# Keeping x on chip after the first mixer, turning some of its quarters through DRAM, and another order of the last HGRN head groups

## The chip, the cores and the metric

The kernel runs on one core of one Trainium2 chip. The metric is the time of one execution on the device in microseconds (us). The program does its matrix products on TensorE (PE), element-wise work on VectorE (DVE) and ScalarE (ACT), small work and part of the transfers on GpSimd (POOL), and issues the weight transfers from SyncE (SP). SBUF is the memory on the chip, PSUM the memory that TensorE writes into, and DRAM the memory beside the chip.

## What is computed

A trunk of two layers on 256 rows of 2048 columns, all in float32. Layer 0 mixes the rows with a gated DeltaNet (GDN), layer 1 with HGRN2; each mixer is followed by a SwiGLU feed-forward block (FFN) with 5632 inner columns. Each of the four sub-layers normalizes its input by rows and adds its result to x:

```python
h = x
for layer in range(DEPTH):
    if layer % N_MIXERS == 0:
        h = h + gdn_mixer(rmsnorm(h, gdn_norm[j]), gdn_w_in[j], gdn_conv[j], gdn_a_log[j], ...)
    else:
        h = h + hgrn2_mixer(rmsnorm(h, hgrn_norm[j]), hgrn_w_in[j], lb_table[layer], ...)
    h = h + swiglu(rmsnorm(h, ffn_norm[layer]), ffn_w_gate[layer], ffn_w_up[layer], ffn_w_down[layer])
return rmsnorm(h, final_norm)

def swiglu(h, w_gate, w_up, w_down):
    return (jax.nn.silu(h @ w_gate) * (h @ w_up)) @ w_down

def hgrn2_mixer(h, w_in, lower_bound, head_norm, w_out):
...
    o = hgrn2_chunked(q, k, i, logf).astype(h.dtype)
    o = rmsnorm(o, head_norm) * jax.nn.silu(gate)
    return o.reshape(B, S, HGRN_VAL_DIM) @ w_out
```

## The kernel before

**Weights and the main stream.** All weights are read once, as halves of 128x1024 float32 (512 KB), by SP's queue into `raw`. Each half is split into two numbers of lower precision: ACT writes the rounded part `wh`, DVE the rest `wl` (`load` in `stream`, lines 610 to 623). The activations are split likewise (`xt_h` and `xt_l` for the input of a sub-layer, `ot_h` and `ot_l` for the output of a mixer, `hth` and `htl` inside the FFN), and a product is formed as xh·wh + xh·wl + xl·wh. One half so feeds twelve matmuls of 128x512, called *main* below. Halves are loaded three ahead and have four buffers at each step.

**Groups.** A `Group` is a run of halves that add up into one PSUM tile, with a function `end` that takes the result out. In order of time: the GDN mixer with its out projection, FFN 0, the HGRN mixer with its out projection, FFN 1. An FFN is 12 gate-and-up groups of 96 mains, four down groups of 144 mains (one for each quarter of 512 columns of x), 10 more gate-and-up groups, and four down groups of 120 mains. HGRN takes its 16 heads in four head groups; each has the groups f, q, v and z of 96 mains, in the order f0 q0 v0 z0 f1 ... z3 (lines 1638 and 1639). An out projection is done in parts (four for GDN, two for HGRN); each part is four groups of 48 mains, one for each quarter. The part p reads head groups 2p and 2p+1, the first in the first 24 mains of a group and the second in the last 24.

**x and the boundaries.** x lives in DRAM as `x_home`. Where a group adds to a quarter of it, `load_x` (line 777) brings the quarter into one of two buffers, `add_x` (line 781) adds the PSUM tile on DVE, and the quarter is stored again; both transfers are POOL's. At the three boundaries (GDN to FFN 0, FFN 0 to HGRN, HGRN to FFN 1) `next_input` (line 789) then makes the input of the next sub-layer from each quarter: `make_xt` (line 731) does eight transposes of 128x128 on TensorE into PSUM, four splits on ACT (`xt_h`, with the norm's weight as scale) and four on DVE (`xt_l`); `sumsq` (line 696) sums the squares on ACT. The row scale of the norm is applied later, behind the products.

**Turning through DRAM.** In HGRN and in the FFN a second way to transpose is in use, `turn` (line 751): DVE turns all 32x32 blocks of a 128x1024 tile, POOL stores the result to DRAM (`rows`), and four loads of POOL bring it back with the blocks at their places (`turned`). HGRN's f and q come through it (`blocks_in`, `rows_in`), and so does the output of a head group (`head_out`, line 1207): `zs` gets the gated output, is turned by way of the buffer of `v`, and is split into `ot_h` and `ot_l`, which have three buffers.

**HGRN's work beside the stream.** `hgrn_scores` (line 1452) makes the score tile `sc` and the tile `cross` of a head group with some 30 element-wise steps and small matmuls; `hgrn_o` (line 1589) multiplies them with `v`, and `head_out` follows.

**What sets the order.** Nothing is issued as it is written. `Recorder.add` collects all operations, and `plan` (line 311) puts them in order with a model: a cost for each operation (`COST`), landing times for transfers, and a latest time for each, counted back from those that use it. The main matmuls keep the order in which they were written. The others are placed between them by their latest time; small matmuls and transposes (tiles called `aux`) go between mains where the model has their inputs ready with a slack of 1.5 us. Each engine then works in the planned order and waits in it, POOL with its transfers too. All operations are issued by one line, 502, so the profile names them by their tiles.

Of the kernel before, what the change touches and what calls it, by code (L numbers as in the profile page):

```python
# [8 lines left out]
F32 = mybir.dt.float32  # L9
F32R = mybir.dt.float32r  # L10
U8 = mybir.dt.uint8
AF = mybir.ActivationFunctionType
ALU = mybir.AluOpType
# [4 lines left out]
P = 128  # L18
# [7 lines left out]
N_HGRN = 4  # L26
# [9 lines left out]
    "k0 k1 k2 k3 v0 v1 z0 z1 v2 z2 k4 k5 v3 z3 v4 k6 o0 k7 v5 z4 z5 o1 v6 v7 z6 z7 o2 o3"  # L36
)

# [477 lines left out]
class Trunk:  # L519
# [211 lines left out]
    def make_xt(self, cg, norm):  # L731
# [11 lines left out]
        for pair, ps in enumerate(two):  # L743
            for k in range(2):
# [3 lines left out]
                    self.norms[:, norm, 4 * cg + kt : 4 * cg + kt + 1],  # L748
                )

    def turn(self, x, blocks, turned, by_head=False):

        nc = self.nc
        width = x.shape[1] // 4
        if by_head:
            b, rows = (x.rearrange(e, t=2, n=4, c=4) for x, e in ((blocks, "p (c n t j) -> p t n c j"), (x, "p (t n c i) -> p t n c i")))
            for tt in range(2):
                nc.vector.transpose(b[:, tt], rows[:, tt])
        else:
            nc.vector.transpose(  # L760
                blocks.rearrange("p (c a j) -> p a c j", c=4, j=32), x.rearrange("p (a c i) -> p a c i", c=4, i=32)
            )
        rows = self.tile(self.dram, [4, P, width], f"rows{width}", bufs=3)
        nc.gpsimd.dma_start(rows.rearrange("c p a -> p c a"), blocks.rearrange("p (c a) -> p c a", c=4))
        for c in range(4):
            nc.gpsimd.dma_start(
                turned[32 * c : 32 * c + 32].rearrange("i (q a) -> i q a", q=4),
                rows[c].rearrange("(q i) a -> i q a", q=4),
            )
        return turned  # L770

    def x_cols(self, x, cg):
        if x is self.a["x"]:
            return x[cg]
        return x.rearrange("(t p) c -> p t c", p=P)[:, :, cg * 512 : (cg + 1) * 512]

    def load_x(self, cg):
        self.x[cg] = self.tile(self.xpool, [P, 2, 512], "x", ordered=True)
        self.nc.gpsimd.dma_start(self.x[cg], self.x_cols(self.x_at, cg))

    def add_x(self, ps, cg, keep=True):
        x = self.x[cg]
        self.nc.vector.tensor_tensor(out=x, in0=x, in1=ps, op=ALU.add)
        if keep:
            self.nc.gpsimd.dma_start(self.x_cols(self.x_home, cg), x)
        if cg == 3:
            self.x_at = self.x_home

    def next_input(self, norm, row):


        def after(cg):
            self.make_xt(cg, norm)
            self.sumsq(cg)
            if cg == 3:
                self.make_rstd(row)

        return after
# [3 lines left out]
    def ffn(self, j, after):  # L802
        nc, a = self.nc, self.a
        hts = {}

        def gate_up(gi):
            def end(ps):
                h1 = self.tile(self.pool, [P, 2, T], "h1", bufs=4)
                for tt in range(2):
                    col = self.rstd[:, tt : tt + 1]  # L810
                    sg = self.tile(self.pool, [P, T], "sg", bufs=2)
                    nc.scalar.activation(sg, ps[:, tt, 0:T], AF.Silu, scale=col)
                    nc.vector.scalar_tensor_tensor(
                        out=h1[:, tt, :], in0=ps[:, tt, T:512], scalar=col, in1=sg,
                        op0=ALU.mult, op1=ALU.mult,
                    )
                blocks = self.tile(self.pool, [P, 512], "blocks", bufs=2)
                flat = h1.rearrange("p t c -> p (t c)")
                turned = self.turn(flat, blocks, flat).rearrange("p (q a j) -> p a q j", q=4, j=32)
                hts[gi] = ht, lt = tuple(  # L820
                    self.tile(self.pool, [P, 2, 2, P], f"ht{x}", F32R, bufs=max(FF_PARTS)) for x in "hl"
                )
                as_turned = lambda x: x.rearrange("p t n (q j) -> p (t n) q j", q=4)
                nc.scalar.activation(as_turned(ht), turned, AF.Copy)
                nc.vector.tensor_tensor(
                    out=as_turned(lt), in0=turned, in1=as_turned(ht.bitcast(F32)), op=ALU.subtract
                )

            gu = a[f"ffn_gu{j}"]
            return Group(  # L830
                [gu[gi, i] for i in range(4)],
                lambda ps, i, h, l: self.mm_rows(ps, i, h, l, 4, self.operand), end,
            )

        def down(part, cg):
            first = sum(FF_PARTS[:part])
            n = FF_PARTS[part] // 2
            w = a[f"ffn_d{j}_{part}"]

            def operand(kt):  # L840
                h, l = hts[first + kt // 2]
                return h[:, :, kt % 2, :], l[:, :, kt % 2, :]

            last = part == len(FF_PARTS) - 1
            apart = last and j == 1 and cg == 3

            def end(ps):
                if apart:
                    self.finish_last(ps)
                    return  # L850
                self.add_x(ps, cg, not (last and j == 1))
                if last:
                    after(cg)

            mm = self.mm_apart if apart else self.mm_rows
            return Group(
                [w[cg, i] for i in range(n)],
                lambda ps, i, h, l: mm(ps, i, h, l, n, operand), end,
                lambda: self.load_x(cg), apart,
            )  # L860

        groups = []
        for part, n in enumerate(FF_PARTS):
            lo = sum(FF_PARTS[:part])
            groups += [gate_up(gi) for gi in range(lo, lo + n)]
            groups += [down(part, cg) for cg in range(4)]
        groups[0].begin = lambda: self.enter(f"ffn{j}")
        return groups


# [5 lines left out]
    def gdn_setup(self):  # L876
        nc, a = self.nc, self.a
        self.enter("gdn")
        t = lambda shape, tag, dt=F32: self.tile(self.pool, shape, tag, dt)
        self.conv = t([P, 32, 4], "conv")  # L880
        nc.gpsimd.dma_start(self.conv, a["gdn_conv"])
        self.gate_in = t([64, 2], "gate_in")
        nc.gpsimd.dma_start(self.gate_in, a["gdn_gate"])
        self.gdn_hn = t([P, 33], "gdn_hn")[:, 0:1]
        nc.gpsimd.dma_start(self.gdn_hn, a["gdn_hn"])
        self.unit = t([P, 8, 32], "unit")
        nc.gpsimd.dma_start(self.unit, a["unit"])
        self.expo = t([P, 4], "expo")
        nc.gpsimd.memset(self.expo[:, 0:4:2], 0.5)
        nc.gpsimd.memset(self.expo[:, 1:4:2], -0.5)  # L890
        self.resets = self.tile(self.pool, [64, T], "sq", bufs=2)
        nc.gpsimd.memset(self.resets, 1.0)
        nc.gpsimd.memset(self.resets.rearrange("p (c s) -> p c s", s=CH)[:, :, 0:1], 0.0)
        zero = self.tile(self.pool, [3, 512], "w", bufs=2)
        nc.gpsimd.memset(zero, 0.0)
        self.v_rows = [self.tile(self.dram, [T + 3, 512], f"v_rows{i}", bufs=1) for i in range(2)]
        for rows in self.v_rows:
            nc.gpsimd.dma_start(rows[0:3, :], zero)
        self.gates = t([P, 2, 64], "gates")
        self.shift = t([P, 32, 6], "shift")  # L900
        self.g_rows = self.tile(self.dram, [32, T], "g_rows", bufs=1)
        self.g_tots = self.tile(self.dram, [32, 4], "g_tots", bufs=1)
# [454 lines left out]
    def out_proj(self, name, p, states, last, after):  # L1357
# [8 lines left out]

        def make(cg):
            def end(ps):
                self.add_x(ps, cg)
                if last:  # L1370
                    after(cg)

# [13 lines left out]
    def hgrn_setup(self):  # L1386
        nc, a = self.nc, self.a
        self.enter("hgrn")
        t = lambda shape, tag, dt=F32: self.tile(self.pool, shape, tag, dt)
        self.hgrn_hn = t([P, 25], "hgrn_hn")[:, 0:1]  # L1390
        nc.gpsimd.dma_start(self.hgrn_hn, a["hgrn_hn"])
# [60 lines left out]
    def hgrn_scores(self, g, rows, st):  # L1452
        nc = self.nc
# [29 lines left out]
        for h in range(4):  # L1483
            nc.tensor.matmul(
                ps[:, h * P : (h + 1) * P], kp[:, h, 0:P], qp[:, h, :], start=True, stop=True
            )
        cross = t([P, 512], "cross")
        nc.scalar.activation(cross, ps, AF.Copy)
        st["cross"] = cross

        sc = t([P, 8, P], "sc")
        nc.gpsimd.memset(sc, 0.0)

        sides = (slice(0, CH), slice(CH, P))
# [112 lines left out]
    def hgrn(self, after):  # L1607
# [27 lines left out]
            )  # L1635
            return [rows(1, f_end), rows(0, q_end), rows(2, v_end), rows(3, z_end)]

        for g in range(N_HGRN):
            groups += part(g)
        groups[0].begin = self.hgrn_setup  # L1640
        groups += self.out_proj("hgrn_out", 0, states, False, after)
        groups += self.out_proj("hgrn_out", 1, states, True, after)
# [53 lines left out]
    def run(self):  # L1696
        self.setup()
        self.start(0, True)
        groups = self.gdn(self.next_input(1, False))
        groups += self.ffn(0, self.next_input(2, False))  # L1700
        groups += self.hgrn(self.next_input(3, False))
        groups += self.ffn(1, self.finish)
        self.stream(groups)
        self.leave()

    def enter(self, name):

        self.leave()
        self.pool = self.nc.pool(name, 1, phase=True)

    def leave(self):
        if self.pool:
# [83 lines left out]
```

## Time and profile before

| what | value |
|---|---|
| median of 3 runs | 2775.16 us (2774.61 to 2776.39) |
| the profiled execution, its own time | 2773.76 us |
| its span, first to last instruction | 2772.0 us |
| TensorE transposes of x (`aux<-head,x`) | 112, of these 96 at the boundaries |
| DMA, mean over the span | 222 GB/s, 616.00 MB |
| software queue (POOL's transfers) | 109.48 MB, 13.1% of 16 engines' span |

The profile is one execution on the chip. Its page gives the busy time of each engine, a picture of the span in 40 slices, the queues, the chain of waits that ended last, and the costliest groups of instructions. A group's row names engine, operation, the tile written and the tiles read, the shape, the count, the busy time in us, the mean of one in ns, and the idle time before them with what ended it. In the timeline a row is start, duration, engine, operation, and in brackets the idle time before it and what ended that. PE's matmuls overlap, so their pace is read from start to start. The clock of TensorE is given as a share of full speed.

### The profile page before, as it was taken

What the parts mean: (1) busy time and instruction counts of PE and PEld (TensorE: products, weight loads), DVE (VectorE), ACT (ScalarE), POOL (GpSimd) and SP (SyncE); (2) the same over time, 40 slices, a digit from 0 to 9 for tenths busy, and PEclk for the clock granted to TensorE, in tenths of its full rate; (3) what the DMA queues carried; (4) which work ended last, traced back from release to release, by engine and by line L of the source; (5) the groups of instructions that cost most, each with busy time, mean ns of one, the idle gap of its engine ahead of it and who ended that gap; (6) DMA issues with size and microseconds to landing.
All of it is one profiled execution on the core that took longest, in us unless ns stands there. A gap on an engine that the chain in (4) does not pass through costs nothing.

```text
span 2772.0 us, 39544 instructions
## 1 busy us (share of the span) xinstructions
PE 2753.7 (99%) x14730; PEld 2312.3 (83%) x14730; DVE 1765.3 (64%) x2571; ACT 1435.5 (52%) x2028; POOL 414.2 (15%) x646
## 2 busy tenths in 40 slices
PE   9999999999999999999999999999999999999998
PEld 9988988887888888888888888888788888888887
DVE  6787888878755555445555576787755555455554
ACT  6656666565554444434444466566454444344443
POOL 1212222232111111001110101101111111011100
PEclk9999999999999999999999999999999999999999
DMA  7686668677777667766666767567787667676664
GB/s 256 197 279 209 205 232 265 214 231 240 237 236 227 215 217 221 226 224 216 220 216 223 232 194 224 192 186 229 231 264 217 218 215 226 221 223 217 218 215 159
DMA packets 175841, 616.00 MB, mean 222 GB/s; under 512 B 24618, under 2 KB 25786, under 8 KB 175520
## 3 DMA queue, kind: packets, MB, share of 16 engines
q1 hardware_dynamic: 138912, 503.15, 56.4%
q0 software_dynamic: 36448, 109.48, 13.1%
q8 instruction: 115, 1.88, 0.3%
q10 hardware_dynamic: 288, 0.85, 0.1%
q14 instruction: 78, 0.64, 0.1%
HBM read 568.25 MB, written 45.13 MB: 221 GB/s over the span
## 4 chain that ended last, share of the span: by engine, by line
PE 98%; DVE 1%; ACT 0%; issue 0%; POOLq 0%; POOL 0%; DVEq 0%; ACTq 0%
PE main L502 92%; PE aux L502 7%; DVE wl L502 0%; ACT dec L502 0%; ACT wh L502 0%; DVE ot_l L502 0%; DVE zs L502 0%; DVE utmp L502 0%; DVE u L502 0%; DVE x L502 0%; ACT y L502 0%; ACT xt_h L502 0%; POOLq L1792 0%; ACT junk L502 0%; DVE xl L502 0%
## 5 line engine op out<-in xcount | busy, mean ns | idle before, releaser
L502 DVE TENSOR_TENSOR wl<-raw,wh 128x1024 fp32r<-128x1024 f32 x945 | 1157.6, 1226 | 914.2 <-ACT wh L502 907.0
L502 ACT ACTIVATE wh<-raw 128x1024 fp32r<-128x1024 f32 x945 | 1000.7, 1060 | 1230.3 <-PE main L502 1180.1
L502 PE MATMUL main<-wh,xt_l 128*128 128x512 f32 x2432 | 949.9, 391 | 0.0
L502 PE MATMUL main<-wl,xt_h 128*128 128x512 f32 x2432 | 948.2, 390 | 1.3 <-DVE wl L502 1.3
L502 PE MATMUL main<-wh,xt_h 128*128 128x512 f32 x2432 | 948.2, 390 | 0.0
L502 PEld LDWEIGHTS main<-wl,xt_h 128*128 128x128 f32 x2432 | 456.6, 188 | 96.4 <-DVE wl L502 2.1
L502 PEld LDWEIGHTS main<-wh,xt_l 128*128 128x128 f32 x2432 | 456.7, 188 | 94.0
L502 PEld LDWEIGHTS main<-wh,xt_h 128*128 128x128 f32 x2432 | 456.7, 188 | 93.5
L502 PE MATMUL main<-wh,htl 128*128 128x512 f32 x664 | 258.9, 390 | 0.0
L502 PE MATMUL main<-wl,hth 128*128 128x512 f32 x664 | 258.4, 389 | 0.0
L502 PE MATMUL main<-wh,hth 128*128 128x512 f32 x664 | 258.4, 389 | 0.0
L502 PE MATMUL main<-wh,ot_h 128*128 128x512 f32 x384 | 150.7, 392 | 3.0 <-ACT ot_h L502 3.0
L502 PE MATMUL main<-wh,ot_l 128*128 128x512 f32 x384 | 151.0, 393 | 1.7 <-DVE ot_l L502 1.7
L502 PE MATMUL main<-wl,ot_h 128*128 128x512 f32 x384 | 151.1, 393 | 0.0
L502 PE MATMUL main<-xt_h,wl 128*128 128x256 f32 (+1 forms) x528 | 149.0, 282 | 0.4 <-DVE wl L502 0.4
L502 PE MATMUL main<-xt_l,wh 128*128 128x256 f32 (+1 forms) x528 | 148.4, 281 | 0.0
L502 PE MATMUL main<-xt_h,wh 128*128 128x256 f32 (+1 forms) x528 | 147.5, 279 | 0.0
L502 PEld LDWEIGHTS main<-wh,htl 128*128 128x128 f32 x664 | 124.7, 188 | 26.3 <-DVE htl L502 0.5
L502 PEld LDWEIGHTS main<-wl,hth 128*128 128x128 f32 x664 | 124.7, 188 | 25.8
L502 PEld LDWEIGHTS main<-wh,hth 128*128 128x128 f32 x664 | 124.7, 188 | 25.7
L502 POOL DMA_DIRECT2D rows<-blocks x44 | 33.5, 761 | 648.6 <-DVE blocks L502 612.3
L502 POOL DMA_DIRECT2D h<-rows x176 | 95.8, 551 | 200.0 <-issue 123.9
(214 smaller groups left out, 2383.2 us busy)
## 6 DMA issues: line engine op xcount, KB each, us to landing
raw<-in_ffn_gu SPq DMA_DIRECT2D x352, 512.0 KB, 4.7
raw<-in_ffn_d SPq DMA_DIRECT2D x176, 512.0 KB, 4.6
raw<-in_hgrn_in SPq DMA_DIRECT2D x128, 512.0 KB, 4.6
raw<-in_gdn_kq SPq DMA_DIRECT2D x64, 512.0 KB, 4.9
raw<-in_gdn_v SPq DMA_DIRECT2D x64, 512.0 KB, 4.4
raw<-in_gdn_z SPq DMA_DIRECT2D x64, 512.0 KB, 4.9
raw<-in_gdn_out SPq DMA_DIRECT2D x64, 512.0 KB, 4.8
x_home<-x POOLq DMA_DIRECT2D x36, 512.0 KB, 5.1
```

Of the source, the lines that this page charges most:

```text
L502: getattr(getattr(tc.nc, op.eng), op.method)(*args, **kw)
```

## The change

It has three parts.

- **x stays in SBUF.** When FFN 0 begins, `keep_x` opens a pool `resident` and loads quarters 0 and 1 once from `x_home`; quarters 2 and 3 stay in the two buffers where GDN's last projection left them. From then on `load_x` and the store in `add_x` do nothing. This takes away 22 stores to and 22 loads from `x_home`.
- **Quarters turned through DRAM.** `next_input` gets a number: at the GDN boundary the first 2 quarters, at FFN 0's the first 3, at HGRN's the first 2 go through the new `turn_xt`, which is `turn` (one DVE transpose, one store, four loads), four ACT splits and eight DVE splits, in place of eight TensorE transposes, four ACT and four DVE splits. It uses tiles that exist already in GDN and HGRN (`wide`, `g_row`, `kqv`; `blocks_in`, `q`, `k`) and three new ones in the FFN. `sumsq` is recorded ahead of the transposes.
- **HGRN's order.** f and q of the last two head groups come ahead of v and z of group 2: `f2 q2 f3 q3 v2 z2 v3 z3`. `cross` and `sc` get a second buffer.

```diff
+HGRN_ORDER = "f0 q0 v0 z0 f1 q1 v1 z1 f2 q2 f3 q3 v2 z2 v3 z3"
...
+    def turn_xt(self, cg, norm):
+
+        nc = self.nc
+        x = self.x[cg]
+        spare = lambda i: self.tile(self.pool, [P, 1024], self.spare[i])
+        flat = self.turn(x.rearrange("p t c -> p (t c)"), spare(0), spare(1 + cg % 2))
+        blocks = flat.rearrange("p (q a j) -> p a q j", q=4, j=32)
+        at = lambda out, tt: out[:, tt * P : (tt + 1) * P].rearrange("p (q j) -> p q j", q=4)
+        for k in range(4):
+            col = self.norms[:, norm, 4 * cg + k : 4 * cg + k + 1]
+            h, low = self.xt_h[cg][:, k, :], self.xt_l[cg][:, k, :]
+            nc.scalar.activation(
+                h.rearrange("p (t q j) -> p t q j", t=2, q=4),
+                flat.rearrange("p (q t n j) -> p n t q j", q=4, t=2, n=4)[:, k], AF.Copy, scale=col,
+            )
+            for tt in range(2):
+                nc.vector.scalar_tensor_tensor(
+                    out=at(low, tt), in0=blocks[:, 4 * tt + k], scalar=col,
+                    in1=at(h.bitcast(F32), tt), op0=ALU.mult, op1=ALU.subtract,
+                )
...
+    resident = None
+
+    def keep_x(self):
+
+        self.resident = self.nc.pool("resident", 1, phase=True)
+        for cg in range(2):
+            self.x[cg] = self.tile(self.resident, [P, 2, 512], f"resident{cg}")
+            self.nc.gpsimd.dma_start(self.x[cg], self.x_cols(self.x_home, cg))
+
     def load_x(self, cg):
+        if self.resident:
+            return
...
-    def add_x(self, ps, cg, keep=True):
+    def add_x(self, ps, cg, store=True):
...
-        if keep:
+        if store and not self.resident:
...
-    def next_input(self, norm, row):
+    def next_input(self, norm, row, turned):
...
         def after(cg):
-            self.make_xt(cg, norm)
             self.sumsq(cg)
+            (self.turn_xt if cg < turned else self.make_xt)(cg, norm)
...
-        groups[0].begin = lambda: self.enter(f"ffn{j}")
+        def begin():
+            self.enter(f"ffn{j}", j == 0)
+            self.spare = ("x_blocks", "x_turned0", "x_turned1")
...
+        self.spare = ("wide", "g_row", "kqv")
...
-                self.add_x(ps, cg)
+                self.add_x(ps, cg, cg < 2 or not last)
...
+        self.spare = ("blocks_in", "q", "k")
...
-        cross = t([P, 512], "cross")
+        cross = t([P, 512], "cross", bufs=2)
...
-        sc = t([P, 8, P], "sc")
+        sc = t([P, 8, P], "sc", bufs=2)
...
-        for g in range(N_HGRN):
-            groups += part(g)
+        parts = [part(g) for g in range(N_HGRN)]
+        groups += [parts[int(n)]["fqvz".index(kind)] for kind, n in HGRN_ORDER.split()]
...
-        groups = self.gdn(self.next_input(1, False))
-        groups += self.ffn(0, self.next_input(2, False))
-        groups += self.hgrn(self.next_input(3, False))
+        groups = self.gdn(self.next_input(1, False, 2))
+        groups += self.ffn(0, self.next_input(2, False, 3))
+        groups += self.hgrn(self.next_input(3, False, 2))
```

How the planned order moves is shown at three places. A row is the line, the operation, the tile written and the tiles read with the planner's numbers, the shape, and the count. The first is TensorE in the last part of GDN's out projection, 12 to 14 mains into the third quarter's group (`main_8565`). Before, the second quarter (`x_8463`) is transposed there by `head`, which holds the unit matrix:

```order
L502 MATMUL main_8565<-wh_8499,ot_l_8118 128x512
L502 MATMUL main_8565<-wh_8528,ot_h_8111 128x512
L502 MATMUL main_8565<-wl_8538,ot_h_8111 128x512
L502 MATMUL aux_8592<-head_58,x_8463 128x128 x4
L502 MATMUL aux_8599<-head_58,x_8463 128x128 x4
L502 MATMUL main_8565<-wh_8528,ot_l_8118 128x512
```

With the change, at the same place (`main_8550`) the mains run on:

```order
L507 MATMUL main_8550<-wl_8507,ot_h_8111 128x512
L507 MATMUL main_8550<-wh_8498,ot_l_8118 128x512
L507 MATMUL main_8550<-wh_8513,ot_h_8111 128x512
L507 MATMUL main_8550<-wl_8523,ot_h_8111 128x512
L507 MATMUL main_8550<-wh_8513,ot_l_8118 128x512
```

The set of eight transposes is gone from the stream; the one of the third quarter, a group later, is still there. The second place is TensorE at the products of the last head group, `hgrn_o(3)`, with its tiles `v`, `sc` and `cross`. Before, they stand 28 mains into the second group of HGRN's first out projection, where the mains read `ot`:

```order
L502 MATMUL main_17682<-wh_17664,ot_l_14102 128x512
L502 MATMUL main_17682<-wh_17664,ot_h_14101 128x512
L502 MATMUL aux_17771<-v_17308,sc_16922 128x128 x4
L502 MATMUL aux_17780<-v_17308,cross_17419 128x128
L502 MATMUL aux_17780<-v_17308,sc_16922 128x128
```

With the change they stand 20 mains into the group z3, where the mains still read `xt`:

```order
L507 MATMUL main_17477<-wh_17433,xt_l_16_72 128x512
L507 MATMUL main_17477<-wh_17433,xt_h_12_68 128x512
L507 MATMUL main_17477<-wl_17449,xt_h_12_68 128x512
L507 MATMUL aux_17517<-v_17490,sc_16008 128x128 x4
L507 MATMUL aux_17522<-v_17490,cross_17043 128x128
L507 MATMUL aux_17522<-v_17490,sc_16008 128x128
```

They moved forward by 152 mains. The third place is POOL at the end of HGRN. `ocol` is the scale of a head group's output, `rows<-v` and `zs<-rows` turn the output of a head group, `x_home` is x in DRAM. Before, the turn of group 3 (`rows<-v_17308`) stands among stores and loads of x:

```order
L502 DMA x_home_96<-x_13948 128x2x512
L502 DMA x_17774<-x_home_96 128x2x512
L502 TENSOR_TENSOR ocol_17834<-so_17782,neghalf_60 128x8
L502 DMA x_home_96<-x_14255 128x2x512
L502 DMA x_17906<-x_home_96 128x2x512
L502 DMA rows_2882_17914<-v_17308 128x4x256
L502 DMA x_home_96<-x_17774 128x2x512
L502 DMA zs_17502<-rows_2882_17914 32x4x256 x4
L502 DMA x_17993<-x_home_96 128x2x512
L502 DMA x_home_96<-x_17906 128x2x512
L502 DMA x_18053<-x_home_96 128x2x512
```

With the change there are the turns of groups 2 and 3 one behind the other, and then those of the first two quarters of x at the boundary (`blocks_in`, `q`, `k`):

```order
L507 TENSOR_TENSOR ocol_17388<-so_17293,neghalf_60 128x8
L507 DMA rows_2822_17499<-v_16944 128x4x256
L507 DMA zs_17142<-rows_2822_17499 32x4x256 x4
L507 TENSOR_TENSOR ocol_17581<-so_17526,neghalf_60 128x8
L507 DMA rows_2881_17767<-v_17490 128x4x256
L507 DMA zs_17678<-rows_2881_17767 32x4x256 x4
L507 DMA rows_2949_18098<-blocks_in_18086 128x4x256
L507 DMA q_18153<-rows_2949_18098 32x4x256 x4
L507 DMA rows_2965_18183<-blocks_in_18170 128x4x256
L507 DMA k_18240<-rows_2965_18183 32x4x256 x4
```

The transfers of x left POOL's queue here, and two turns of x came in behind the turns of the head groups.

More of the change, by code (lines that the diff above doesn't have):

```diff
@@ L850, in end @@
                     return
-                self.add_x(ps, cg, not (last and j == 1))
+                self.add_x(ps, cg)
                 if last:
@@ L866, in ffn @@
             groups += [down(part, cg) for cg in range(4)]
-        groups[0].begin = lambda: self.enter(f"ffn{j}")
+        def begin():
+            self.enter(f"ffn{j}", j == 0)
+            self.spare = ("x_blocks", "x_turned0", "x_turned1")
+        groups[0].begin = begin
         return groups
@@ L1704, in run, with enter @@
         self.leave()
-    def enter(self, name):
+        self.nc.close(self.resident)
+    spare = None
+    def enter(self, name, resident=False):
         self.leave()
+        if resident:
+            self.keep_x()
         self.pool = self.nc.pool(name, 1, phase=True)
+        if resident:
+            self.nc.edge(self.resident.phase, self.pool.phase)
     def leave(self):
```

## The prediction

> **What bounds the kernel now.** I read the page first, for the engine that is busy all the time, then the chain of waits, then what that engine waited for, and last its timeline where it waited. The page and the view of the core's clock:
>
> ```profile
> PE 2753.7 (99%) x14730; PEld 2312.3 (83%) x14730; DVE 1765.3 (64%) x2571; ACT 1435.5 (52%) x2028; POOL 414.2 (15%) x646
> core 0: 2772.0 us, clock 0.999
> PE 98%; DVE 1%; ACT 0%; issue 0%; POOLq 0%; POOL 0%; DVEq 0%; ACTq 0%
> ```
>
> TensorE is busy for 99% of the span at nearly full clock and holds 98% of the chain. So a change gains only by taking instructions off TensorE or by ending one of its few waits, and loses only by making a new one. The waits of TensorE, as total, times and longest, then its timeline at the two longest:
>
> ```profile
> PE main L502 <- ACT ot_h L502: 3.0, 2, 2.2
> PE main L502 <- DVE ot_l L502: 1.7, 2, 1.1
> PE main L502 <- DVE wl L502: 1.7, 3, 0.8
> PE aux L502 <- POOL ones L502: 1.1, 1, 1.1
> PE aux L502 <- DMA first<-in_x: 0.8, 1, 0.8
> 1997.95 0.39 PE L502 MATMUL main<-wh,ot_l 128*128 128x512 f32 x1
> 2000.53 0.50 PE L502 MATMUL main<-wh,ot_h 128*128 128x512 f32 x1 [2.19 <-ACT ot_h L502]
> 2000.87 0.39 PE L502 MATMUL main<-wl,ot_h 128*128 128x512 f32 x1
> 2002.33 0.50 PE L502 MATMUL main<-wh,ot_l 128*128 128x512 f32 x1 [1.07 <-DVE ot_l L502]
> 2002.67 0.40 PE L502 MATMUL main<-wh,ot_h 128*128 128x512 f32 x1
> ```
>
> These five rows are all its waits on others: 8.3 us. The longest ot_h and ot_l waits lie together at 2000 us, where the last HGRN output projection first reads head group 3. That is the place the new HGRN order moves. The pace of the stream without any wait comes from the chain of the whole run, and the cost of a set of transposes from the chain at the GDN to FFN0 boundary:
>
> ```profile
> 800.82 0.87 PE aux L502 x8
> 801.69 10.90 PE main L502 x48
> 812.59 0.87 PE aux L502 x8
> 837.01 636.63 PE main L502 x2808
> ```
>
> A main matmul takes 636.63/2808 = 0.2267 us in the stream, and eight transposes 0.87. From one set to the next is 812.59 - 800.82 = 11.77, of which 48 mains are 48 x 0.2267 = 10.88: a set costs **0.89 us** with its two turns between streams.
>
> **Part 1, the transposes.** Seven quarters (2 + 3 + 2) no longer pass through TensorE, so 56 of the 112 such transposes go:
>
> ```profile
> L502 PE MATMUL aux<-head,x 128*128 128x128 f32 x112 | 14.5, 272 | 0.0
> ```
>
> Each of the seven sets stood in the stream with nothing to hide it: 7 x 0.89 = **6.2 us** gained. The five sets that stay (2, 1, 2) cost what they did; moving the last one from 14 to 32 mains into the next group changes no count.
>
> What is added lies on other engines. Per quarter there is one DVE transpose of 128x1024, a store and four loads on POOL's queue, four ACT and eight DVE splits in place of four and four. The prices, from the same or the nearest forms:
>
> ```profile
> L502 DVE STREAM_TRANSPOSE v<-zs 128x1024 f32<-128x1024 f32 x4 | 5.0, 1242 | 0.1
> L502 DVE SCALAR_TENSOR_TENSOR zs<-aux,ocol,zs 128x128 f32<-128x128 f32 x96 | 29.0, 344 | 0.2
> L502 DVE SCALAR_TENSOR_TENSOR xt_l<-aux,head,xt_h 128x256 fp32r<-128x256 f32 x64 | 26.5, 476 | 7.9 <-ACT xt_h L502 7.9
> L502 ACT ACTIVATE xt_h<-aux,head 128x256 fp32r<-128x256 f32 x64 | 24.9, 473 | 3.2 <-PE aux L502 3.1
> L502 DVE TENSOR_TENSOR wl<-raw,wh 128x1024 fp32r<-128x1024 f32 x945 | 1157.6, 1226 | 914.2 <-ACT wh L502 907.0
> L502 DVE TENSOR_TENSOR x<-x,main 128x1024 f32<-128x1024 f32 x39 | 47.6, 1220 | 17.6 <-PE main L502 17.2
> ```
>
> DVE gains 1.24 + 8 x 0.344 - 4 x 0.476 = 2.1 us of work a quarter, about one weight split more. DVE does one 1.23 us weight split per 12 mains, that is per 2.72 us, so at the boundaries it has the room. The cover is the time from a quarter's last main to the first matmul that reads it. At the GDN and HGRN boundaries the second quarter is the tighter of the two: 96 mains of the last two quarters, 24 of the new stage and one set, 120 x 0.2267 + 0.87 = **28.1 us**. At the FFN0 boundary the quarters are 120 mains long, and the third still has 168 x 0.2267 = 38.1 us. What a turn through DRAM takes:
>
> ```profile
> rows<-blocks_in POOLq DMA_DIRECT2D x8, 512.0 KB, 4.6
> rows_in<-rows POOLq DMA_DIRECT2D x32, 128.0 KB, 5.9
> 1581.27 0.77 POOL L502 DMA_DIRECT2D rows<-blocks_in  x1 [13.68 <-DVE blocks_in L502]
> 1586.63 2.19 POOL L502 DMA_DIRECT2D rows_in<-rows  x4 [4.58 <-DMA rows<-blocks_in]
> ```
>
> Undisturbed it is 0.77 + 4.58 + 2.19 + 5.9 = 13.4 us; the slowest, below, 18.9. Of the 28.1 us, 0.40 + 1.22 go to the add of x, 1.24 to the DVE transpose, and at most 4 x 0.344 x 2 + 0.47 + 1.23 = 4.5 to the splits with a weight split between them. That leaves **20.7 us** for the turn: 7.3 to spare typically, 1.8 with the slowest. POOL's queue works in order, and behind each added store stand the store and the reload of x that remain in GDN:
>
> ```profile
> 799.20 0.72 POOL L502 DMA_DIRECT2D x_home<-x  x1 [4.59 <-DVE x L502]
> 806.55 0.73 POOL L502 DMA_DIRECT2D x<-x_home  x1 [6.62 <-DMA x_home<-x]
> 810.97 0.72 POOL L502 DMA_DIRECT2D x_home<-x  x1 [3.70 <-DVE x L502]
> ```
>
> The first quarter's loads now queue behind a reload that waits until 806.55 for its own store and issues until 807.3; the second's stand likewise behind the next reload. The turn's store, issued some 1.24 after 799.20, lands at about 800.4 + 0.77 + 4.58 = 805.8, so the reload costs 1.5 us of the spare time. I take **nothing** for the added work, since the typical turn leaves 7.3. The ends: 0, as TensorE waits for nothing at these places before, and, if both second quarters took the slowest turn, such a reload and a weight split ahead of the DVE transpose, 2 x (18.9 + 1.5 + 1.23 - 20.7) = +1.9 us.
>
> [...]
>
> **Part 2, x kept in SBUF.** It takes 22 of 36 stores and 22 of 36 loads off POOL and DRAM. In the waits of TensorE none of them appears, so by itself I take nothing; the most that less traffic could give is the 1.7 us that weight splits (wl) were waited for. It also frees POOL at the HGRN end, which part 3 uses.
>
> **Part 3, the HGRN order.** How head group 3 comes late, on POOL, DVE and ACT:
>
> ```profile
> 1970.95 1.66 POOL L502 TENSOR_TENSOR ocol<-so,neghalf 128x8 f32<-128x8 f32 x1 [7.33 <-DVE so L502]
> 1979.23 1.25 DVE L502 STREAM_TRANSPOSE v<-zs 128x1024 f32<-128x1024 f32 x1
> 1980.78 0.77 POOL L502 DMA_DIRECT2D rows<-v  x1 [2.24 <-DVE v L502]
> 1989.87 2.21 POOL L502 DMA_DIRECT2D zs<-rows  x4 [5.58 <-DMA rows<-v]
> 1999.34 1.13 ACT L502 ACTIVATE ot_h<-zs,hgrn_hn 128x1024 fp32r<-128x1024 f32 x1
> 2000.61 1.67 DVE L502 SCALAR_TENSOR_TENSOR ot_l<-zs,hgrn_hn,ot_h 128x256 fp32r<-128x256 f32 x4
> ```
>
> From the end of the DVE transpose (1980.48) to ot_h (1999.34) is 18.9 us, the slowest turn of the trace. The stall is what the starts exceed 0.2267 by: 2.58, 0.34, 1.46 and 0.34 less 4 x 0.2267, so 2.35 + 0.11 + 1.23 + 0.11 = **3.8 us**. In the new order hgrn_o(3) stands 20 mains into z3 instead of 76 mains behind its end, 152 x 0.2267 = 34.5 us earlier. What is late next is the buffer: ot has three, and group 3 takes that of group 0, which the first projection reads until 48 mains (10.9 us) before group 3 is needed. After that come ot_h 1.13 and ot_l 1.67, with at most one weight split ahead of each (1.06 on ACT, 1.23 on DVE) and 0.4 of hand-over: 5.5 us, so 5.4 to spare. I take the whole **3.8 us** as gained. Its bounds: 0 if something else holds group 3 up, and 3.8, since no more stands there.
>
> What pays is that scores for groups 2 and 3 now follow each other closely while DVE is already nearly full. The busiest stretch of HGRN before, as busy time of PE, PEld, DVE, ACT and POOL:
>
> ```profile
> 1836.00:1858.00 22.00, 22.00 (x251) 18.39 (x250) 20.01 (x28) 14.94 (x22) 0.00 (x0) 1.00 0.48 156
> ```
>
> DVE is 20.01/22.00 = 91% busy there, and TensorE still loses nothing. I estimate some 95% over the packed groups. The weight splits go first when they are due, so what slips is a score product, and a set of those standing in the stream waits for its input. Bounds: 0, and a stall like that of 2000 us, 3.8. I take 0, since the 91% stretch cost nothing.
>
> **Sum.** -6.2 - 3.8 = -10.0 us on the profiled execution of 2773.76 (span 2772.0 and 1.76 around it): 2763.8. That execution lies 1.40 under the median of the runs shown, so on their scale 2775.16 - 10.0 = **2765.2 us**. With its bounds (-1.7, the wl waits; +1.9, the slow turns) it lies in 2763.5 to 2767.
>
> **The rivals.**
> 1. *The transposes go, the HGRN gain does not come*: a packed score product stalls TensorE about as long as ot_h and ot_l did, or group 3 is late again. For it: the 91% row, and two more buffers don't make DVE faster. Against it: that row cost nothing, and none of the five waits is a score product's. 2775.16 - 6.2 = 2769.0, and 2767 to 2771 about it, a weight split's length and a half either way.
> 2. *Turned quarters come a little late* at the GDN and HGRN boundaries, by 1 to 5 us each: about 2770 (5 us lost in all), up to 2775. For it: the 18.9 us turn with 1.8 us to spare.
> 3. *They come very late*, the slower side. The place is the first matmul of a new stage that reads the second quarter, at both boundaries. At this one place the loads of the turn land late, because POOL works in order and each of its waits for a landing holds up all behind it. Every microsecond of a turn beyond 20.7 is paid twice. The gain is used up at a turn of 20.7 + 10.0/2 = 25.7 us, and slower by over 0.2% (5.55 us) from 20.7 + 15.5/2 = 28.5. A turn of 30 us gives 2765.2 + 2 x 9.3 = 2783.8. For it: the 6.62 us that POOL stood waiting at 806.55. Against it: the slowest turn seen, with x traffic in POOL's queue, took 18.9, and at the HGRN boundary that traffic is gone.
>
> [...]
>
> **How the numbers follow.** Chances: forecast 0.70, rival 1 0.18, rival 2 0.06, rival 3 0.06. A measurement of this kernel can tell about 0.2%, 5.55 us, from no change, so faster means under 2769.6. The forecast and half of rival 1 lie there: 0.79. The other half and rival 2 are within 0.2%: 0.15. Rival 3 is slower: 0.06. The range runs from 2762.5, the forecast's lower end less 1 for the spread of the runs shown (2774.61 to 2776.39), to 2770.5, which takes in most of rival 1.
>
> **What would show it.** Sets of eight transposes of x: 14 before, 7 after. No gap of TensorE at the first mains reading the second quarter, nor at its first reading of ot in the last projection. If a gap stands at the boundaries, released by xt_h or xt_l, rivals 2 or 3 hold; if a new gap stands inside v2 to z3, released by DVE or ACT, rival 1. I am wrong in the sum if the 7 sets show less than 0.85 us each, or if waits in GDN before 797 us move, whose code does not change.

## The result, and the profile after

The changed kernel takes **2763.25 us** (median of 5 runs, 2763.11 to 2764.88) where the kernel before takes 2775.16 beside it (5 runs, 2774.61 to 2776.68): a ratio of 0.9957, interval 0.9943 to 0.9972. The forecast was 2765.2, so the change gained 11.9 us in place of 10.0. The profiled execution took 2763.11 us, with a span of 2761.4, 10.6 less than before. From its page, and then its waits of TensorE (total, times, longest):

```profile
PE 2746.1 (99%) x14674; PEld 2305.2 (83%) x14674; DVE 1777.0 (64%) x2606; ACT 1437.8 (52%) x2029; POOL 402.6 (15%) x637
```

```profile
PE aux L507 <- DMA first<-in_x: 1.4, 1, 1.4
PE main L507 <- DVE wl L507: 1.3, 2, 0.8
PE aux L507 <- POOL ones L507: 1.1, 1, 1.1
PE main L507 <- ACT ot_h L507: 0.8, 1, 0.8
PE main L507 <- DVE ot_l L507: 0.6, 1, 0.6
```

TensorE has 56 instructions less. The wait of 2.2 us for ot_h is gone, no score product (`sc`, `cross`) is waited for, and no `xt_h` or `xt_l`. The chain of waits at the end of HGRN is one run of mains with two sets of transposes in it, where there was a stall and four sets. Before (rows between are left out), then after:

```profile
1998.38 1.06 ACT wh L502
2001.00 1.28 DVE ot_l L502 x3
2010.79 0.87 PE aux L502 x8
2022.57 0.87 PE aux L502 x8
2034.35 0.87 PE aux L502 x8
2046.12 0.87 PE aux L502 x8
```

```profile
1989.93 33.78 PE main L507 x149
2023.71 0.87 PE aux L507 x8
2024.58 15.00 PE main L507 x66
2039.58 0.87 PE aux L507 x8
2040.45 9.76 PE main L507 x43
```

Where the 10.6 us went shows when the 12024 mains are numbered and the start of the same main is compared in both traces:

| stretch | after less before, us | what it is |
|---|---|---|
| start, to 244 us | -0.85 | loads of the first inputs; nothing changed here |
| 244 to 796 | 0.0 | GDN |
| GDN to FFN 0 | -1.79 | 2 sets of transposes, 0.89 each |
| FFN 0 to HGRN | -2.68 | 3 sets |
| HGRN's f, q, v, z and first out projection | +0.30 | the same 1088 small matmuls in 23 pieces, not 22 |
| HGRN's last out projection | -3.83 | the stall |
| HGRN to FFN 1 | -1.78 | 2 sets |
| FFN 1 | 0.0 | |

The change itself makes 6.25 + 3.83 - 0.30 = 9.8 of this; the start differs by chance from one execution to the next (in e8 and e10 below, which are one kernel, it differs by 1.7 us). Two questions were left: what had made the stall, and how much of their cover the turned quarters use.

### The profile page after: what moved, and what is told of

Same layout as the page of the kernel before. It is cut to its first block, busy times and chain, and to the rows that moved or that the text cites. A ratio compares the mean times of both kernels' runs of the same rounds, so it can differ in the third digit from the quotient of the medians.

```text
span 2761.4 us, 39441 instructions
## 1 busy us (share of the span) xinstructions
PE 2746.1 (99%) x14674; PEld 2305.2 (83%) x14674; DVE 1777.0 (64%) x2606; ACT 1437.8 (52%) x2029; POOL 402.6 (15%) x637
## 4 chain that ended last, share of the span: by engine, by line
PE 98%; DVE 1%; ACT 0%; issue 0%; DMA 0%; SPq 0%; POOLq 0%; POOL 0%; DVEq 0%; ACTq 0%
PE main L507 92%; PE aux L507 6%; DMA raw<-in_gdn_kq 0%; DVE wl L507 0%; ACT dec L507 0%; ACT wh L507 0%; SPq L507 0%; DVE zs L507 0%; DVE utmp L507 0%; DVE u L507 0%; DVE x L507 0%; ACT y L507 0%; POOLq L1842 0%; DVE ot_l L507 0%; ACT junk L507 0%
```

## The experiments

**Which part earns what.** Four kernels do single parts of the change. e1 is the kernel before with the new HGRN order alone:

```diff
+HGRN_ORDER = "f0 q0 v0 z0 f1 q1 v1 z1 f2 q2 f3 q3 v2 z2 v3 z3"
...
-        cross = t([P, 512], "cross")
+        cross = t([P, 512], "cross", bufs=2)
...
-        sc = t([P, 8, P], "sc")
+        sc = t([P, 8, P], "sc", bufs=2)
...
-        for g in range(N_HGRN):
-            groups += part(g)
+        parts = [part(g) for g in range(N_HGRN)]
+        groups += [parts[int(n)]["fqvz".index(kind)] for kind, n in HGRN_ORDER.split()]
```

> The kernel before with HGRN's new order and the second buffers of cross and sc, and nothing else. Theory (the prediction's part 3: the place of hgrn_o(3) is what made the stall at 2000 us): the stall goes, -3.8 us, about 2771.4. Rival (the turn of head group 3 was slow because stores and reloads of x stand in POOL's queue and share the DMA engines with it): the x traffic is still there, so the turn stays near 18.9 us, but it starts earlier and the buffer of ot is now what it waits for; if that traffic decides, part of the stall stays and less than 2 us is gained, 2773 or more.

Measured: 2769.64 against 2774.96, ratio 0.9982 (0.9973 to 0.9990). In the trace the last out projection is 3.83 us shorter and what stands ahead of it in HGRN 0.30 longer, with all of x's traffic on POOL's queue. The order ends the stall; the rival falls.

e2 is the changed kernel without its other two parts, so x stays in SBUF and all else is as before:

```diff
-HGRN_ORDER = "f0 q0 v0 z0 f1 q1 v1 z1 f2 q2 f3 q3 v2 z2 v3 z3"
+HGRN_ORDER = "f0 q0 v0 z0 f1 q1 v1 z1 f2 q2 v2 z2 f3 q3 v3 z3"
...
-        cross = t([P, 512], "cross", bufs=2)
+        cross = t([P, 512], "cross")
...
-        sc = t([P, 8, P], "sc", bufs=2)
+        sc = t([P, 8, P], "sc")
...
-        groups = self.gdn(self.next_input(1, False, 2))
-        groups += self.ffn(0, self.next_input(2, False, 3))
-        groups += self.hgrn(self.next_input(3, False, 2))
+        groups = self.gdn(self.next_input(1, False, 0))
+        groups += self.ffn(0, self.next_input(2, False, 0))
+        groups += self.hgrn(self.next_input(3, False, 0))
```

> The kernel before with x kept in SBUF, and nothing else (no quarter turned through DRAM, the old HGRN order). Theory (part 2 of the prediction: worth nothing by itself): 2775.2, the stall at 2000 us stays at 3.8 us. Rival (POOL's x traffic made the last turn slow): hgrn_o(3) still stands 28 mains into the second output group, but the turn takes 13.4 us in place of 18.9, which is 5.5 us sooner and more than the 3.8 us of the stall: it goes, about 2771.4.

Measured: 2774.84 against 2774.96, ratio 1.0000 (0.9991 to 1.0009). Nothing is gained, as the prediction said, but not for its reason. The rival was half right: the turn did become faster. POOL's timeline, and the time to landing of the four loads (lowest, median, highest):

```profile
1979.71 0.79 POOL L507 DMA_DIRECT2D rows<-v  x1 [8.16 <-DVE v L507]
1987.13 2.18 POOL L507 DMA_DIRECT2D zs<-rows  x4 [6.62 <-DMA rows<-v]
DMA to landing us min/median/max: 4.6/4.9/5.9
```

The last load was issued at 1988.8 and had landed by 1994.7. Yet ot_h ran no earlier in the program. ACT's timeline:

```profile
1994.60 1.06 ACT L507 ACTIVATE wh<-raw 128x1024 fp32r<-128x1024 f32 x1 [1.66 <-PE main L507]
1997.32 1.06 ACT L507 ACTIVATE wh<-raw 128x1024 fp32r<-128x1024 f32 x1 [1.66 <-PE main L507]
1998.28 1.13 ACT L507 ACTIVATE ot_h<-zs,hgrn_hn 128x1024 fp32r<-128x1024 f32 x1
```

ACT stood idle for 1.66 us before 1997.32 with the input of ot_h at hand, because a weight split stood ahead of ot_h in its queue, and that split waited for TensorE to free a buffer. So a new theory: the *place* of ot_h in ACT's order made the stall. e5 tests it in e2's kernel by moving ot_h and ot_l one weight half forward, through the landing time that the planner assumes; on ACT and DVE nothing else changes its place:

```diff
-LANDING_OF = {"wide": 7.0, "u": 7.0}
+LANDING_OF = {"wide": 7.0, "u": 7.0, "zs": 5.5}
```

> The kernel of e2 (before, with x resident) with one swap: the planner is told a landing of 5.5 us in place of 6.5 for the loads of the head groups' output, which changes one place in the order, ot_h and ot_l of head group 3 one weight half earlier on ACT and DVE. Theory (new, after e2: ot_h stood in ACT's queue behind a weight split that waited for TensorE, so the place in the order made the stall, not the transfer, which had landed by 1994.7): ot_h runs at about 1995.7, ot_l ends at about 1998.6, some 1.0 us of the 3.8 stays, 2.8 gained, about 2772. Rival (the transfer's landing, or the splits of ot themselves, set the time): the stall stays as in e2, 2774.8.

Measured: 2770.82 against 2774.84, ratio 0.9984 (0.9975 to 0.9993). In the trace 2.71 us of the stall are gone:

```profile
1995.47 1.06 ACT L507 ACTIVATE wh<-raw 128x1024 fp32r<-128x1024 f32 x1 [1.66 <-PE main L507]
1996.43 1.14 ACT L507 ACTIVATE ot_h<-zs,hgrn_hn 128x1024 fp32r<-128x1024 f32 x1
1998.19 1.06 ACT L507 ACTIVATE wh<-raw 128x1024 fp32r<-128x1024 f32 x1 [0.62 <-PE main L507]
```

ot_h now goes ahead of that split, and TensorE waits only 0.98 for ot_l. e6 makes the same swap in the kernel before, where x's traffic remains:

> The kernel before with the swap of e5 alone; x goes through DRAM as before. Theory: both limits lie close here, the order first and the landing of the turn (about 1997.9) just behind it. With the swap ot_h starts at the landing, ends at 1999.1, ot_l at 2000.8: 0.9 + 1.3 = 2.2 us of stall stay, 1.6 gained, about 2773.4. Rival (only the order counts): 2.8 gained as in e5, about 2772.

Measured: 2772.26 (2770.19 to 2778.01), ratio 0.9993 (0.9984 to 1.0002), so unclear by the times. In the trace the two waits are 2.00 and 1.14 us where they were 2.35 and 1.24: only 0.45 us less, so 3.1 stay where 2.2 had been expected. The transfer is now the limit: the last load landed at 1998.71 and ot_h started at 1998.82. In the kernel before it landed at 1997.88, and ot_h started 1.5 us later, at 1999.34. But e6's trace is one of its slower executions (2774.49); its two fastest runs, 2770.19 and 2770.23, are as fast as e5. That the landing, a little earlier there, makes the difference is likely but not shown, as only one execution has a trace. So two things held the stall up, the place first and the landing 0.4 to 1.5 us behind it: taking away the slow transfer alone (e2) shows nothing, taking away the bad place alone (e6) a part that varies from run to run, and both together (e5) most of it. The new order passes both, since the whole chain starts 152 mains sooner.

e3 turns 2, 3 and 2 quarters with the old order, and x goes through DRAM as before. Beside the order's lines of e2, it differs from the changed kernel in the following (two small pieces, for the last store of x and the end of the pool, are left out):

```diff
-            self.enter(f"ffn{j}", j == 0)
+            self.enter(f"ffn{j}")
...
-                self.add_x(ps, cg, cg < 2 or not last)
+                self.add_x(ps, cg)
```

> The kernel before with 2, 3 and 2 quarters turned through DRAM, and nothing else (x stored and reloaded at every boundary, the old HGRN order). Theory: 7 sets of transposes less, -6.2 us, and the stall at 2000 us stays: 2769.0. Rival (turned quarters come late when POOL also carries x at all three boundaries): a wait of 1 to 5 us for xt_h or xt_l at the GDN and HGRN boundaries, 2771 to 2779.

Measured: 2770.62, but from 2767.75 to 2775.09; ratio 0.9984 (0.9976 to 0.9993). The seven sets are gone from the trace and the stall stands, as the theory says. The rival is right in one place, in another form: behind the HGRN boundary the last transposes on TensorE wait for the add of x, and 1.0 us is lost. The wait of TensorE, then ACT and DVE (rows between are left out):

```profile
PE aux L507 <- DVE x L507: 0.8, 1, 0.8
2038.45 1.31 ACT L507 ACTIVATE xt_h<-k,head 128x256 fp32r<-128x256 f32 x3 [4.14 <-DMA k<-rows]
2038.99 1.40 DVE L507 SCALAR_TENSOR_TENSOR xt_l<-k,head,xt_h 128x128 fp32r<-128x128 f32 x5 [3.43 <-ACT xt_h L507]
2042.67 1.22 DVE L507 TENSOR_TENSOR x<-x,main 128x1024 f32<-128x1024 f32 x1
```

The reload of x was not late: it had landed by 2032.8. The add stood in DVE's queue behind the splits of the turned quarter `k`, and these waited for the turn, which took 21.2 us from the issue of its store (2017.10) to its last landing (2038.34). In the changed kernel, without x's traffic, the same turn takes 15.0 (2013.50 to 2028.50). That is what x in SBUF is worth beside the turns. e4 is the changed kernel with no quarter turned (`next_input` with 0, 0, 0):

> The changed kernel with no quarter turned through DRAM (x resident and the new HGRN order stay). Theory: the 3.8 us of the stall at 2000 us are gained and the 6.2 us of the seven sets are not: 2771.4. Rival (the transposes on TensorE were hidden or cheaper than 0.89 us a set): within 2 us of the changed kernel, 2765 or less.

Measured: 2770.00, ratio 0.9981 (0.9973 to 0.9990). The trace has the 3.83 and the 0.30 of e1 and none of the 6.25.

**How much cover is left.** In the trace after, the second quarter at the GDN boundary, on POOL, ACT and PE:

```profile
811.52 0.76 POOL L507 DMA_DIRECT2D rows<-wide  x1 [1.57 <-DVE wide L507]
819.10 0.71 POOL L507 DMA_DIRECT2D x<-x_home  x1 [6.81 <-ACT xt_h L507]
821.33 2.22 POOL L507 DMA_DIRECT2D kqv<-rows  x4 [1.52 <-DMA rows<-wide]
830.76 1.31 ACT L507 ACTIVATE xt_h<-kqv,head 128x256 fp32r<-128x256 f32 x3 [2.05 <-DMA kqv<-rows]
837.43 1.03 PE L507 MATMUL aux<-head,x 128*128 128x128 f32 x8
```

From the end of the DVE transpose (811.23) to ACT's first split are 19.5 us; the store alone landed 9.5 us after its issue, at 821.05, beside x's own store and reload. The set at 837.43 stands 32 mains into the stage, so the first main that needs the quarter is at 837.4 - 8 x 0.2267 = 835.6, about 4 us after its first split; the last of its twelve splits ended at 835.07, 0.5 us ahead. e7 lengthens the way:

```diff
-        flat = self.turn(x.rearrange("p t c -> p (t c)"), spare(0), spare(1 + cg % 2))
+        there = self.tile(self.dram, [P, 1024], "there", bufs=2)
+        back = spare(1 + cg % 2)
+        nc.gpsimd.dma_start(there, x.rearrange("p t c -> p (t c)"))
+        nc.gpsimd.dma_start(back, there)
+        flat = self.turn(back, spare(0), back)
```

> The changed kernel with one more trip of each turned quarter through DRAM ahead of its turn (a store and a load of 512 KB on POOL's queue, about 0.8 + 5.2 + 0.7 + 6.1 = 12.8 us; same result). Theory (the cover of 28.1 us is nearly used up: by the trace the second quarter was ready 3.4 us ahead of its first use at the GDN boundary and 4.8 at HGRN's): late by 9.4 and 8.0 us, 17 us lost, about 2780. Rival (the spare time is larger than it looks, since the splits were put late by the planner and not by the landing): under 4 us lost, 2767 or less.

Measured: 2777.40 (2774.98 to 2779.62), ratio 1.0010 (1.0001 to 1.0019): slower than the kernel before, and 14 us above the changed one. Both waits are there:

```profile
PE main L507 <- ACT xt_h L507: 5.6, 2, 3.2
PE aux L507 <- DVE x L507: 2.6, 2, 1.3
```

4.7 us are lost at the GDN boundary and 6.9 at HGRN's, less than the 9.4 and 8.0 expected, and not all of it by the late quarter: at each boundary 1.8 us go to the transposes of the last quarter, which the planner now puts right behind that quarter's last main, so that they wait for the add of x (the second row). At GDN the added trip moved the turn's store back by 13.6 us, but the turn itself was 4 us shorter: no reload of x was in flight beside its loads, and they landed within 6.3 us in place of 9.4.

The other side is to turn more. e8 and e10 are one kernel on two chips, 3, 3 and 3 quarters, e11 has 3, 4 and 3, e12 all; e9 is the changed kernel itself:

> The changed kernel with three quarters turned through DRAM at all three boundaries (3, 3, 3 in place of 2, 3, 2). Theory: two more sets leave TensorE, -1.8 us; the third quarter's cover at GDN and HGRN is 96 mains, 21.8 us, and the way takes 1.6 + 2.5 + 13.4 to 19.5 + 1.2, so it is in time at HGRN and 0 to 3 us late at GDN: 2761.5 to 2765. Rival (a wait at both, with the pause of TensorE followed by a lower clock): 2766 or more.

> The changed kernel itself, beside the next three on the same chip. Theory (the trace accounts for 6.3 + 3.5 us; what the medians show beyond it is the start, which differs by some 2 us from run to run, and the lower clock that follows a pause of TensorE, which this kernel no longer has): its runs lie close together, within 3 us, and its median is 10 to 12 us under the kernel before. Rival (a further gain that no row shows): 13 us or more under it.

> The kernel of e8 beside the changed kernel on the same chip. Theory: in e8's trace no wait was added and 1.8 us were gained behind the start, so 1.8 us under e9 in the lowest runs; but the third quarter came without time to spare (first split at 842.8, first use about 842.9), so some runs wait and the scatter is wider. Rival (in time in every run): median 1.8 under e9 with its scatter.

> As e10, with the fourth quarter turned as well at the FFN 0 boundary (3, 4, 3). Theory: its cover is only 72 mains, 16.3 us, and the way takes 1.6 + 1.2 + 13.4 + 1.2 = 17.4 or more: a wait of 1 to 3 us against 0.9 gained, so 0 to 2 us above e10, and a lower clock behind the wait may add 2. Rival (in time): 0.9 under e10.

> All quarters turned through DRAM at all three boundaries (4, 4, 4); no transpose of x is left on TensorE behind the start. Theory: 4.5 us of sets gained against the changed kernel, but the last quarter has 16.3 us of cover at every boundary and waits on POOL's queue behind the one before: late by 1 to 3 us at FFN 0 and HGRN and 3 to 8 at GDN, with lower clocks behind: 2764 to 2773, wide scatter. Rival (the turns keep up): 2759.

| kernel | quarters | median (lowest to highest), us | pause longest in its trace, us |
|---|---|---|---|
| e9, the change | 2, 3, 2 | 2763.53 (2763.15 to 2763.82) | 0.98, in GDN |
| e8 | 3, 3, 3 | 2763.82 (2762.57 to 2767.92) | 0.98, in GDN |
| e10 | 3, 3, 3 | 2766.65 (2763.24 to 2769.96) | 0.98, in GDN; 0.95 for xt_h |
| e11 | 3, 4, 3 | 2767.31 (2764.64 to 2771.82) | 3.65 for xt_h |
| e12 | 4, 4, 4 | 2778.96 (2774.41 to 2781.23) | 2.59 for xt_h |

A pause is what the distance from one main's start to the next exceeds 0.2267 by. e8's trace has the 1.8 us of two more sets and no wait; in e10's the third quarter comes late at the GDN boundary, and half its runs are 6 us slower. On ACT of e10 the split waits for the turn's loads:

```profile
841.78 1.71 ACT L507 ACTIVATE xt_h<-g_row,head 128x256 fp32r<-128x256 f32 x4 [1.85 <-DMA g_row<-rows]
```

e11 lies within what was expected, e12 above it, with 8.7 us of waits for xt_h at five places:

```profile
PE main L507 <- ACT xt_h L507: 8.7, 5, 2.4
PE main L507 <- DVE xt_l L507: 1.5, 4, 0.4
```

So no version that was run beats the change. At GDN's boundary the cover reaches safely for two quarters (the third waits in e10 and e11) and at FFN 0's for three (TensorE waits 1.7 us for the fourth in e11). At HGRN's it reaches further: the third quarter is in time in all three traces that turn just three there (e8, e10 and e11 gain 2.67 us at that boundary in place of 1.78). 2, 3 and 3 quarters, some 0.9 us better by these traces, were not tried.

## Why the prediction was right, point by point

- **The seven sets.** Forecast 6.2, measured 6.25 (1.79 + 2.68 + 1.78). e4 without them loses this in its trace.
- **The stall.** Forecast 3.8, measured 3.83, with 0.30 given back, which the sum lacked: the price of the new order stood at zero. It is no wait: a piece of 112 small matmuls, which held the mains up for 3.03 us, became two of 48 and 64, which take 1.61 and 1.63; that is 0.21 of it, and the rest lies in the pace of the mains around such pieces. DVE, at 91% before and 94% after (20.76 of the 22 us from 1830), held nothing up.
- **The stall's cause was misread.** The prediction laid it to the turn of 18.9 us. But the last load had landed 17.4 us after the DVE transpose, and for the other 1.5 us ot_h stood behind a weight split, which the chain of the kernel before names (`ACT wh` at 1998.38). e2, e5 and e6 show two limits close together; the transfer alone was not enough. The forecast survived since the new order moves the start of the chain and so passes both. That step, followed through, would have given x in SBUF alone most of the 3.8 us, which e2 does not show.
- **x in SBUF is worth nothing by itself.** Right (e2), though that no wait named it was no sufficient reason. Beside the turns it is worth 1.0 us: without it the second turn at HGRN's boundary takes 21.2 us in place of 15.0 (e3).
- **The cover.** Forecast 7.3 us to spare in the typical case and 1.8 with the slowest turn. The second quarter at GDN took 19.5, longer than the slowest turn seen before. Of the 20.7 us that the prediction left for it 1.2 remained, and its last split ended 0.5 us ahead of the first main that reads the quarter. The room was there, but the typical turn of 13.4 was the wrong row for a store that runs beside two transfers of x and lands 9.5 us after its issue in place of 4.58, and the nothing in the sum was nearer to its limit than it says.
- **Rival 3 is real.** A longer turn (e7) or a shorter cover (e12) makes the kernel about 0.1% slower than before. In both the mechanism named is there, waits for xt_h of a late quarter; in e7 3.6 of the 11.6 us lost are the planner's new place for other transposes.
- **The size.** The medians gained 11.9 and 11.6 (e9), the trace accounts for 9.8. The sum took the 1.40 us by which the profiled execution lay under the median over to the changed kernel, where it is 0.14. That is 1.26 of the rest, and the start is 0.85. The prediction held nothing for either; the last section has what the runs show of the first.

## What to carry to other kernels

Work moved from TensorE to transfers paid here just what TensorE's instructions had cost, 0.89 us a set, as long as the cover was longer than the slowest way, not only the typical one (19.5 us against 13.4 at GDN's boundary); a third quarter there turned the gain into scatter (2763.24 to 2769.96 in e10), all four at each into a loss (2778.96 in e12). Where an instruction runs late, look first at what stands ahead of it in its own queue: here a split that waited for TensorE held up one whose input had landed 3.6 us before, and making the transfer faster changed nothing. Two limits close together hid each other here (2.71 us of the stall gone with both away in e5, 0.45 and nothing with one in e6 and e2), so take away both before either is called harmless.

## What the runs showed of the hardware that was not expected

TensorE's granted clock fell to 0.50 for 3.41 us behind the stall in e2, and stayed at 1.00 behind the same stall in the kernel before. Windows as long as that drop, from the stall on, as length, busy time of PE, PEld, DVE, ACT and POOL, then the granted clock, DMA share and GB/s; before first, then e2:

```profile
1996.84:2000.25 3.41, 1.50 (x7) 0.92 (x5) 1.92 (x2) 1.87 (x2) 0.00 (x0) 1.00 1.02 402
2000.25:2003.67 3.42, 2.07 (x8) 1.42 (x9) 2.02 (x5) 0.22 (x1) 0.73 (x1) 1.00 0.90 347
2003.67:2007.08 3.41, 3.41 (x17) 2.83 (x16) 1.06 (x1) 1.06 (x1) 0.00 (x0) 1.00 0.55 174
```

```profile
1997.69:2001.10 3.41, 0.73 (x2) 0.30 (x2) 2.69 (x5) 1.72 (x2) 0.00 (x0) 1.00 0.59 187
2001.10:2004.51 3.41, 3.24 (x8) 2.57 (x9) 0.11 (x1) 0.00 (x0) 0.00 (x0) 0.50 0.37 137
2004.51:2007.93 3.42, 3.42 (x17) 2.80 (x16) 1.23 (x1) 1.06 (x1) 0.00 (x0) 1.00 0.00 0
```

Before, TensorE was busy for 1.50 and 2.07 us of the two windows that hold the stall; in e2 it was busy for 0.73 of the one that ends where the clock falls. While the clock is at 0.50, mains in e2's timeline start 0.427 us apart in place of 0.227. e2 lost 1.5 us by it in the stretch whose stall is the same as before's.

A lower clock stands behind pauses in e11 and e12 too. From 845 to 855 us, behind the GDN boundary, the mean granted clock is 0.69 in e11 and 0.86 in e12, where TensorE waited for xt_h at that boundary; in e10, whose pause for xt_h there is 0.95, it is 1.00. What decides whether the clock falls behind a pause is not shown by these rows.

The scatter of the runs differs between kernels with long pauses and those without. The record has the mean granted clock of every run, to three places: the two kernels below with no pause over 0.98 us had 0.999 in all of their runs, which lie within 1.2 us; the three with a pause of 2.00 or 2.35 had less in some or most, and their runs lie within 4.5 to 7.8 us.

| kernel | longest pause, us | lowest to highest, us | runs at a clock of 0.999 |
|---|---|---|---|
| before | 2.35 | 2773.58 to 2778.03 | 4 of 33 |
| e3 | 2.35 | 2767.75 to 2775.09 | 1 of 11 |
| e6 | 2.00 | 2770.19 to 2778.01 | 6 of 11 |
| e1 | 0.98 | 2769.35 to 2770.56 | 11 of 11 |
| e5 | 0.98 | 2770.12 to 2771.30 | 11 of 11 |

The other runs had 0.998 or 0.997. The traces of the kernel before and of e3 are at 0.999, most of their runs are not. The medians of e1, e4, e5 and the change gained 1.3 to 2.1 us more than their traces: 5.3 for 3.5, 5.0 for 3.5, 4.0 for 2.7, 11.6 to 11.9 for 9.8. Against only those runs of the kernel before that had 0.999 (medians 2773.78, 2773.53 and 2773.67 beside e1, e5 and e9, of four, two and one run), e1 gains 4.1, e5 2.7 and e9 10.1, so in these three most of the surplus goes with the clock of the runs compared. What is left is within what the start differs by: the first 244 us lie between 1.1 us under and 1.2 above those of the kernel before.
